# Two output weight tiles split in each block of the input projection instead of three, and one operand for the first half's sums of squares

## The chip, the cores and the metric

The kernel runs on one NeuronCore of a Trainium2 chip. Its engines are TensorE (PE in the profile, with its weight loads as PEld), VectorE (DVE), ScalarE (ACT), GpSimd (POOL) and SyncE (SP). SP issues nearly all DMAs here, in one queue and in order. The metric is device time in microseconds; the median of three runs of the kernel before is 2884.24 us (2881.09 to 2888.12).

## The reference

One inference step of a hybrid encoder layer, in fp32, over 2048 prompt frames and 32 frames of a running stream (2080 tokens), with D_MODEL 1024. A mixer runs stick-breaking attention (8 heads of 64) beside a Mamba-2 SSD (8 heads of 64, state 64, conv 4), both on one input projection; both results are normalised, concatenated and sent through one output projection; a gated conv feed-forward follows.

```python
def mixer(h, k_past, v_past, ssm_h0, conv_prev, p):
    proj = h @ p['w_in']
...
    attn = stick_breaking(q, q_pos, k_all, v_all, k_pos).reshape(b, l, D_ATT)
...
    y, h_fin = ssd_scan(xh, dt, a, bm, cm, ssm_h0.astype(jnp.float32))
...
    y = rmsnorm(y * jax.nn.silu(z), p['g_ssm_out'])
    out = jnp.concatenate([rmsnorm(attn, p['g_attn_out']), y], axis=-1) @ p['w_out']
    return out, k, v, h_fin.astype(ssm_h0.dtype), conv_new

def layer(x, k_past, v_past, ssm_h0, ssm_conv_prev, ffn_conv_prev, p):
    m, k, v, h_fin, ssm_conv_new = mixer(rmsnorm(x, p['g_mix_pre']), k_past, v_past, ssm_h0, ssm_conv_prev, p)
    x = x + rmsnorm(m, p['g_mix_post'])
    f, ffn_conv_new = conv_ffn(rmsnorm(x, p['g_ffn_pre']), ffn_conv_prev, p)
    x = x + rmsnorm(f, p['g_ffn_post'])
```

The change touches `w_out` (the output projection's weights) and the sums of squares of the two norms around `m` (`g_mix_post` and `g_ffn_pre`).

## The kernel before

**Arithmetic.** Every fp32 operand of a large matmul is split into a high and a low part (names ending in hi and lo, or the halves of a tile `w`); each product is three matmuls (hi by hi, hi by lo, lo by hi). So L180 (`dense`) issues three matmuls for each weight block of 128 by 128. Weights are split once: `divide` (L155) takes the raw fp32 tile (`wraw`, loaded in L137), casts the high part on ACT (L160), subtracts on POOL (L161) and stores both to DRAM (L164, `wS_...`). Every later use is a `recall` (L147), a load of the split tile (L152, `w<-wS_...`). `weight` (L122) picks one or the other by whether the key is in `kept`.

**Buffers and queue.** In the input projection the tiles `w` are of 1 MB and rotate through a ring of three buffers; behind it, of 512 KB in a ring of six. A load at the head of SP's queue waits there until its buffer is free, and everything issued behind it waits too.

**Input projection.** `phase_in` works through four blocks s of 512, 512, 512 and 544 tokens. In each: six tiles of conv, B, C and x; then v (L451, four steps b of 128 tokens, five in the last block, 48 matmuls each, copied out in L460, stored as `o_v` in L468 and, split, as `vS` in L476); then four tiles of wk and four of wq, from the ring; then the gate. Beside wk and wq run the SSD steps: step size and decay on DVE (L464 to L496, ending with `da`), cumulative sums on PE (L498, L499, copied to `acum` in L503), transposes (L509, L564, L575), the store of `acT` to `acD` and its broadcast load `acB` (L513, L520), and the products L581 and L593. The squares of the next block's x are added by POOL (L326). Ahead of a step of v, the kernel also splits one of the eight tiles of `wout`, for use in the streams much later; the cast is held behind the last copy of v by `behind`, an order on the engine without a wait.

**Streams.** Afterwards attention runs block by block (`heads`), and each block's tail (`Tail`) is interleaved with the attention of the next one; the last tail runs alone. A tail has two halves of up to 272 tokens. For each, `out_units` runs the eight tiles of the output projection (tile c of `wout`, copied to `m`, squared on ACT into `msq`, summed on POOL in `square`, L875), `residual` normalises and adds x, and `split` prepares the feed-forward. The sums of squares over the 1024 features reach PE as a list of operands of 128 rows: `rstd_steps` issues one matmul by a column of ones (L222) for each operand and each 128 tokens, adding in PSUM. The list is `self.msqs` for the first norm (two operands: `msq`, and the last square `sqt`) and `self.sq` for the second (two operands, `two[0]` with its two halves).

**Order.** The instruction order on each engine is decided by a scheduler from the program's order, its buffers and the explicit orders (`pin`, `behind`, `spaced`). A change of one line can therefore move instructions all over a block.

Of the kernel before, what the change touches and what calls it, by code (L numbers as in the profile page):

```python
# [12 lines left out]
ALU = mybir.AluOpType  # L13
# [21 lines left out]
KC = D // P  # L35
# [234 lines left out]
def phase_in(kn, ctx):  # L270
    nc, tc, a, o = kn.nc, kn.tc, kn.a, kn.o
# [7 lines left out]
    wp = kn.wp  # L279
# [94 lines left out]
    for s, (t0, nt) in enumerate(SBS):  # L374
# [18 lines left out]
        def silu(y, copy):  # L393
            t = tmp.tile([P, 550], F32, name="t")
            kn.behind(nc.scalar.activation(t[:, :W], y, AF.Sigmoid), copy)
            nc.vector.tensor_tensor(y, y, t[:, :W], op=ALU.mult)
# [44 lines left out]
            nc.vector.memset(u[:, 32:40], 0.0)  # L441
        for b in range(nb):
            q = min(P, nt - b * P)
            if 0 < s and 0 < b < 4 and 3 * s + b < KC + 4:
                kn.weight(wp, a["wout"][3 * s - 4 + b], key=("outw", 3 * s - 4 + b))
                kn.behind(kn.cast, copy)
            vp = [psd.tile([P, 512], F32, name="o") for _ in range(2)]
            for h in range(2):
                for k in range(KC):
                    for i, (l, rr) in enumerate(((xhi, wv[0]), (xlo, wv[0]), (xhi, wv[1]))):  # L450
                        nc.tensor.matmul(  # L451
                            vp[h][:q, :260], l[k][:, b * P : b * P + q], rr[:, k, h * 260 : h * 260 + 260],
                            start=i == 0 and k == 0, stop=i == 2 and k == KC - 1,
                        )
            v = sd.tile([P, 520], F32, name="v")
            for dst, src in ((v[:q, 0:260], vp[0][:q, :260]), (v[:q, 260:520], vp[1][:q, :260])):
                if s == 0:
                    copy = nc.scalar.activation(dst, src, AF.Copy, scale=rcol[:q, b : b + 1])
                else:
                    copy = nc.scalar.copy(dst, src)  # L460
            if b == 0:
                for y in owed:
                    silu(y, copy)
            nc.vector.tensor_tensor(  # L464
                u[:q, b * 8 : b * 8 + 8], v[:q, 512:520], kn.cv[:q, C_DTB : C_DTB + 8], op=ALU.add
            )
            tok = t0 + b * P
            nc.sync.dma_start(o["v"][tok : tok + q, :], v[:q, :512])  # L468
            if b == 4:
                nc.sync.dma_start(kn.vF[:], v[:DEC, :512])  # L470
                continue
            vs = sd.tile([P, 2, 512], F32R, name="vs", bufs=1)
            nc.gpsimd.tensor_copy(vs[:, 0, :], v[:, :512])
            nc.gpsimd.tensor_tensor(vs[:, 1, :], v[:, :512], vs[:, 0, :].bitcast(F32), op=ALU.subtract)
            for e in range(2):
                nc.sync.dma_start(  # L476
                    kn.vS[s][:, :, b, e * DH : e * DH + DH].rearrange("h p d -> p h d"),
                    vs[:, e, :].bitcast(F32).rearrange("p (h d) -> p h d", d=DH),
                )
# [512 lines left out]
class Tail:  # L992
# [24 lines left out]
    def out_units(self, s, cat, half):  # L1017

        kn, nc, att = self.kn, self.kn.nc, self.att
        c0, c1 = half  # L1020
        if c0 == 0:
            self.Q = [[self.mp.tile([P, 4, 272], F32, name=f"n{2 * i + e}") for e in range(2)] for i in range(2)]
            self.msq = att.tmp.tile([P, 544], F32, name="sq")
            self.w = {}
        back = list(range(KC - WBUFS * UNIT // KC, KC))
        for i, c in enumerate(range(KC) if c0 == 0 else back + list(range(back[0]))):
            m = self.m(c, half)
            w = self.w.pop(c, None)
            if w is None:
                pool = self.keep if self.keep is not None and c not in back else kn.wp  # L1030
                w = kn.weight(pool, kn.a["wout"][c], key=("outw", c, "part"), tag=f"w{c}" if pool is self.keep else None)
                if c0 == 0 and (c in back or pool is self.keep):
                    self.w[c] = w
            ps = self.po[0].tile([P, 512], F32, name=self.po[1])
            for k in (4, 5, 6, 7, 0, 1, 2, 3):
                kn.dense(ps, w[k : k + 1], cat, c0, c1, k0=k, first=k == 4, last=k == 3, pin=self.pin)
                if k != 3:
                    yield
            nc.scalar.copy(m, ps[:, : c1 - c0])
            if i < KC - 1:  # L1040
                att.square(self.msq[:, c0:c1], m, i == 0)
            else:
                t = att.tmp.tile([P, 272], F32, name="sqt", bufs=2)[:, : c1 - c0]
                nc.scalar.activation(t, m, AF.Square)
                self.msqs = [self.msq[:, c0:c1], t]
            yield
# [5 lines left out]
    def residual(self, s, half):  # L1052

        kn, nc, att = self.kn, self.kn.nc, self.att
        t0 = SBS[s][0]
        c0, c1 = half
        n = c1 - c0
        fast = s in FAST
        rm = kn.rstd_narrow(att.tmp, *kn.bank, self.msqs, n, D, stay=True)
        yield  # L1060
        self.h, two = [], []
        for c in range(KC):
            m = self.m(c, half)
            if c % 2 == 0:
                if self.late:
                    pair = self.late.tile([P, 548], F32, name="xr", bufs=4)
                else:
                    pair = self.yp.tile([P, 548], F32, name="gb") if c % 4 else self.yp.tile([P, 546], F32, name="y")
            x = pair[:, n * (c % 2) : n * (c % 2) + n]
            nc.sync.dma_start(x, kn.a["xT"][:, c, t0 + c0 : t0 + c1])  # L1070
            kn.spaced(nc.vector.scalar_tensor_tensor(
                m, m, kn.col(C_GMIXP + c), rm[:, :n], op0=ALU.mult, op1=ALU.mult
            ), self.pin)
            eng = nc.vector if c % 2 else nc.gpsimd
            h, sq = (x, m) if fast else (m, x)
            eng.tensor_tensor(h, m, x, op=ALU.add)
            nc.sync.dma_start(kn.hS[s][:, c, c0:c1], h)
            nc.scalar.activation(sq, h, AF.Square)
            self.h.append(h)
            if c % 2:  # L1080
                k = c % 4 - 1
                two.append(
                    self.Q[int(c0 > 0)][c // 4][:, k : k + 2, :n] if fast
                    else pair[:, : 2 * n].rearrange("p (k t) -> p k t", k=2)
                )
                if c > 1:
                    eng = nc.vector if fast and c0 and c == KC - 1 else nc.gpsimd
                    eng.tensor_tensor(two[0], two[0], two[-1], op=ALU.add)
            yield
        self.sq = [two[0][:, k, :] for k in range(2)]  # L1090

    def split(self, s, half):


        kn, nc, att = self.kn, self.kn.nc, self.att
        c0, c1 = half
        if c0 == 0:
            self.x = self.cat
        hi, lo = self.x
        for k in range(KC):  # L1100
            m = self.m(k, half)
            nc.scalar.activation(hi[k][:, c0:c1], m, AF.Copy, scale=kn.col(C_GFFN + k))
            kn.spaced(nc.vector.scalar_tensor_tensor(  # L1103
                lo[k][:, c0:c1], m, kn.col(C_GFFN + k), hi[k][:, c0:c1].bitcast(F32),
                op0=ALU.mult, op1=ALU.subtract,
            ), self.pin)
            yield
# [420 lines left out]
def build(nc, tc, a, o):  # L1528
    kn = Kernel(nc, tc, a, o)
    with ExitStack() as ctx:  # L1530
# [17 lines left out]
        with ExitStack() as c2:  # L1548
            kn.wp, kn.unit, kn.wbufs, kn.rbufs = c2.enter_context(tc.tile_pool(name="weights_in", bufs=1)), KC, 3, 2
            rest = phase_in(kn, c2)  # L1550
# [123 lines left out]
```

## Time and profile before

| | before |
|---|---|
| median of 3 runs | 2884.24 us |
| profiled execution | 2887.35 us |
| its span, first to last instruction | 2885.6 us |
| mean granted TensorE clock | 0.984 |
| HBM read, written | 482.40 MB, 156.57 MB |
| input projection, about | first 600 us of the span |

How to read the lines below: in the profile's groups and timelines a row names the start in us, the length, the engine (SPq is SP issuing a DMA), the line, the operation, the tile written and the tiles read, and a count; a bracket holds the idle time ahead of it and what ended it. A row of the list of waits is "engine, tile and line <- what it waited for: us in total, times, longest". A row of the chain of waits gives start, length and what took that stretch on the way to the end of the window. A row of the DMA list ends in KB and the median of the microseconds from issue to landing. `x19` counts instructions put together in one row.

### The profile page before, as it was taken

Reading aid. Unit: us, or ns where it says so; the run is one execution under the profiler, and the core shown is the slowest. Engines: PE = TensorE matmul, PEld = TensorE weight load, DVE = VectorE, ACT = ScalarE, POOL = GpSimd, SP = SyncE. Lnnn points to the kernel's source line nnn. Section 1 sums busy time; section 2 is a strip of 40 time slices with the busy share of each in tenths; the row PEclk is TensorE's granted clock in tenths of the full one; section 3 lists DMA queues with packets and bytes.
Section 4 is the critical chain, followed back from the end, with each engine's and each line's share of the span. In section 5 each row is a group of like instructions: output and inputs, shape, how many; then the busy total and the mean of one; then the engine's idle time right before and its main releaser. Section 6 shows DMA issues by size and latency. Waiting matters only on the chain.

```text
span 2885.6 us, 46011 instructions
## 1 busy us (share of the span) xinstructions
PE 2780.3 (96%) x16709; PEld 2401.0 (83%) x16709; DVE 1643.5 (57%) x2628; ACT 1217.0 (42%) x2568; POOL 1134.0 (39%) x1065
## 2 busy tenths in 40 slices
PE   7998999998999999999999999989999999999997
PEld 6777878986878888897888888878888879899997
DVE  7684747367464454558455555875666653623333
ACT  5343434347555454455333335644444433321111
POOL 4633242325566665556232224453323234411113
PEclk9999999999999999999999999999999999999999
DMA  8969595987768777886655556655555555755556
GB/s 295 290 248 332 199 315 194 280 276 252 249 206 281 275 265 257 268 268 217 201 180 183 175 180 237 206 191 185 176 168 171 167 187 175 247 179 179 167 179 200
DMA packets 348483, 642.02 MB, mean 222 GB/s; under 512 B 73338, under 2 KB 192770, under 8 KB 338530
## 3 DMA queue, kind: packets, MB, share of 16 engines
q1 hardware_dynamic: 348258, 639.09, 67.3%
q8 instruction: 133, 2.18, 0.3%
q14 instruction: 92, 0.75, 0.1%
HBM read 482.40 MB, written 156.57 MB: 221 GB/s over the span
## 4 chain that ended last, share of the span: by engine, by line
PE 79%; DMA 8%; DVE 7%; issue 2%; SPq 2%; POOL 1%; ACT 1%; DVEq 0%; ACTq 0%; POOLq 0%
PE o L180 41%; PE u L180 12%; PE t L180 10%; PE z L914 4%; PE pa L955 4%; PE pt L933 4%; PE o L451 2%; DMA acB<-acD 1%; DMA w<-wS_outw 1%; DVE prow L762 1%; DMA w<-wS_wk 1%; DMA w<-wS_up 1%; DVE f L1431 1%; DVE xlo L1103 1%; DMA k<-kS 1%
## 5 line engine op out<-in xcount | busy, mean ns | idle before, releaser
L180 PE MATMUL o<-xhi,w 128*128 128x512 f32 (+2 forms) x3968 | 1040.9, 344 | 26.3 <-ACT xhi L353 7.8
L180 PEld LDWEIGHTS o<-xhi,w 128*128 128x128 f32 x3968 | 694.9, 190 | 119.4 <-ACT xhi L353 7.8
L180 PE MATMUL o<-xlo,w 128*128 128x512 f32 (+2 forms) x1984 | 681.4, 344 | 5.1 <-DVE xlo L1103 2.2
L767 POOL TENSOR_TENSOR beta<-beta,prow 128x512 f32<-128x512 f32 (+3 forms) x256 | 255.5, 999 | 512.3 <-DVE prow L762 444.0
L180 PEld LDWEIGHTS o<-xlo,w 128*128 128x128 f32 x1984 | 377.1, 190 | 50.5 <-DVE xlo L1103 3.3
L180 PE MATMUL u<-xhi,w 128*128 128x512 f32 x1056 | 351.4, 398 | 0.0
L180 PE MATMUL o<-ah,w 128*128 128x512 f32 x992 | 342.1, 402 | 6.4 <-DVE f L1399 6.3
L1351 POOL TENSOR_TENSOR y<-y,gb 128x512 f32<-128x512 f32 (+1 forms) x88 | 116.1, 1320 | 460.6 <-ACT gb L1350 460.4
L938 DVE TENSOR_TENSOR wt<-pt,wt 128x512 fp32r<-128x512 f32 (+2 forms) x320 | 192.2, 602 | 182.9 <-ACT wt L937 181.0
L161 POOL TENSOR_TENSOR w<-wraw,w 128x512 fp32r<-128x512 f32 (+3 forms) x178 | 245.4, 1380 | 129.2 <-ACT w L160 105.4
L762 DVE TENSOR_TENSOR_SCAN prow<-gam,prow,z 128x513 f32<-128x513 f32 x192 | 245.2, 1277 | 54.3 <-ACT beta L760 53.6
L937 ACT CAST wt<-pt 128x512 fp32r<-128x512 f32 (+2 forms) x320 | 167.7, 525 | 233.1 <-PE pt L933 231.2
L180 PEld LDWEIGHTS u<-xhi,w 128*128 128x128 f32 x1056 | 199.0, 189 | 46.3
L180 PEld LDWEIGHTS o<-ah,w 128*128 128x128 f32 x992 | 186.7, 188 | 48.4 <-DVE f L1399 7.4
L180 PE MATMUL u<-xlo,w 128*128 128x512 f32 x528 | 209.3, 396 | 0.0
L759 ACT ACTIVATE gam<-z 128x512 f32<-128x512 f32 (+2 forms) x320 | 173.1, 541 | 60.7 <-PE z L914 35.2
L180 PE MATMUL t<-xhi,w 128*128 128x272 f32 x960 | 190.4, 294 | 7.6 <-DMA w<-wS_up 4.6
L180 PE MATMUL o<-al,w 128*128 128x512 f32 x496 | 196.6, 396 | 0.0
L933 PE MATMUL pt<-ident,beta 128*128 128x128 f32 x1088 | 184.6, 278 | 0.4 <-DVE wt L938 0.4
L955 PE MATMUL pa<-wt,v 128*64 128x256 f32 (+3 forms) x1152 | 173.5, 281 | 9.8 <-DVE wt L938 5.1
L160 ACT CAST w<-wraw 128x512 fp32r<-128x512 f32 (+3 forms) x178 | 113.0, 635 | 159.9 <-PE o L180 89.3
L1343 DVE SCALAR_TENSOR_TENSOR y<-gb,cv,y 128x512 f32<-128x512 f32 (+1 forms) x176 | 144.0, 818 | 63.9 <-ACT y L1341 60.8
(288 smaller groups left out, 4845.0 us busy)
## 6 DMA issues: line engine op xcount, KB each, us to landing
w<-wS_up SPq DMA_DIRECT2D x264, 512.0 KB, 3.6
w<-wS_dn SPq DMA_DIRECT2D x144, 384.0 KB, 3.4
w<-wS_outw SPq DMA_DIRECT2D x94, 512.0 KB, 6.2
wS_up<-w SPq DMA_DIRECT2D x88, 512.0 KB, 3.4
wraw<-wup SPq DMA_DIRECT2D x88, 256.0 KB, 4.4
k<-kS SPq DMA_DIRECT2D x80, 256.0 KB, 3.5
v<-vS SPq DMA_DIRECT2D x80, 256.0 KB, 3.7
w<-wS_bx SPq DMA_DIRECT2D x18, 1024.0 KB, 5.5
```

The costliest lines, as they stand in the source:

```text
L161: nc.gpsimd.tensor_tensor(lo, raw[:, :m, :], hi.bitcast(F32), op=ALU.subtract)
L180: mm = nc.tensor.matmul(ps[:, : c1 - c0], l, r, start=first and i == 0 and k == 0, stop=last and i == 2 and k == len(w) - 1, **({"skip_gro ...
L759: nc.scalar.activation(g[:, c0:512], z, AF.Sigmoid, scale=-0.125)
L762: nc.vector.tensor_tensor_scan(back(pr), back(g), z[:, 0:1].to_broadcast([P, n + 1]), self.kn.ones[:, 0:1] if prev is None else prev, op0= ...
L767: eng.tensor_tensor(b[:, :n], b[:, :n], pr[:, c0 + 1 : 513], op=ALU.mult)
L914: mm = nc.tensor.matmul(z[:, :n], q[:, P * b : P * b + P], k[:, :n], start=e == 0, stop=e == 1 and kc < s)
L933: mm = nc.tensor.transpose(t[:, P * j : P * j + P], w[:, P * j : P * j + P], kn.ident[:])
L937: nc.scalar.copy(hi, t)
L938: kn.exit = nc.vector.tensor_tensor(lo, t, hi.bitcast(F32), op=ALU.subtract)
L955: nc.tensor.matmul(av[:m, 2 * P * p + c0 : 2 * P * p + 2 * P], v[:, j, :m], wt[:, rest, j, c0:], start=kc == s and p + j + rest == 0, stop ...
L1343: nc.vector.scalar_tensor_tensor(y[:, :W], gb[:, i : i + W], kn.col(wc + i), y[:, :W], op0=ALU.mult, op1=ALU.add)
L1351: nc.gpsimd.tensor_tensor(y[:, :W], y[:, :W], t, op=ALU.mult)
```

## The change

Two edits.

1. In `phase_in`, blocks 1, 2 and 3 each split two tiles of `wout`, ahead of steps 1 and 2 of v: tiles 0 and 1, 2 and 3, 4 and 5. Before, blocks 1 and 2 split three each and block 3 two, all eight. Tiles 6 and 7 now have no key in `kept` when the first stream reaches them, so `weight` sends their four halves through `divide` there: a load of the raw half (prefetched), a cast, a subtraction and a store (`wS_outw_part`), where four recalls stood. Later streams recall those halves.
2. In `out_units`, for the first half of a stream (`c0 == 0`), the last square too is added to `msq` by `square`, so `msqs` is one operand. In `residual`, for the first half, POOL adds the second half of `two[0]` to the first, and `self.sq` is one operand. The second half of each stream is as before. This takes 18 matmuls of L222 away in the four streams and adds eight additions on POOL.

```diff
@@ -441,8 +441,8 @@
         for b in range(nb):
             q = min(P, nt - b * P)
-            if 0 < s and 0 < b < 4 and 3 * s + b < KC + 4:
-                kn.weight(wp, a["wout"][3 * s - 4 + b], key=("outw", 3 * s - 4 + b))
+            if 0 < s and 0 < b < 3:
+                kn.weight(wp, a["wout"][2 * s - 3 + b], key=("outw", 2 * s - 3 + b))
                 kn.behind(kn.cast, copy)
@@ -1037,8 +1037,9 @@
             nc.scalar.copy(m, ps[:, : c1 - c0])
-            if i < KC - 1:
+            if i < KC - 1 or c0 == 0:
                 att.square(self.msq[:, c0:c1], m, i == 0)
+                self.msqs = [self.msq[:, c0:c1]]
             else:
                 t = att.tmp.tile([P, 272], F32, name="sqt", bufs=2)[:, : c1 - c0]
@@ -1088,6 +1089,10 @@
         self.sq = [two[0][:, k, :] for k in range(2)]
+        if c0 == 0:
+            nc.gpsimd.tensor_tensor(self.sq[0], self.sq[0], self.sq[1], op=ALU.add)
+            del self.sq[1]
+            yield
```

The order of instructions moves with it. On SP, in block 1 from v's first stores on, before (`wS_outw_0_1926` and `wS_outw_0_1993` are the first two split tiles, `wS_wk_0_1074` and `wS_wk_0_1117` tiles 0 and 1 of wk):

```order
L476 DMA vS_87<-vs 128x8x64 x2
L468 DMA o_v<-v 128x512
L164 DMA wS_outw_0_1926<-w 128x2048
L137 DMA wraw<-wout 128x1024
L476 DMA vS_87<-vs 128x8x64
L164 DMA wS_outw_0_1993<-w 128x2048
L468 DMA o_v<-v 128x512
L152 DMA w<-wS_wk_0_1074 128x2048
L137 DMA wraw<-wout 128x1024
L476 DMA vS_87<-vs 128x8x64
L152 DMA w<-wS_wk_0_1117 128x2048
```

The same stretch now:

```order
L476 DMA vS_87<-vs 128x8x64 x2
L152 DMA w<-wS_wk_0_1074 128x2048
L468 DMA o_v<-v 128x512
L164 DMA wS_outw_0_1926<-w 128x2048
L137 DMA wraw<-wout 128x1024
L476 DMA vS_87<-vs 128x8x64
L164 DMA wS_outw_0_1993<-w 128x2048
L468 DMA o_v<-v 128x512
L137 DMA wraw<-wout 128x1024
L152 DMA w<-wS_wk_0_1117 128x2048
L476 DMA vS_87<-vs 128x8x64
```

The load of wk's tile 0 has moved from behind both stores to ahead of them, straight behind v's first two stores; that of tile 1 has moved ahead of one vS. Block 2 has the same two stretches with other numbers.

On PE, in block 1 at the end of wk's tile 0 (its 24 matmuls end with `xhi_1620` and `xlo_1628`), before:

```order
L180 MATMUL o<-xhi_1619,w 128x512
L498 MATMUL st<-da,triu 128x32
L499 MATMUL st<-da,ones 128x32
L180 MATMUL o<-xlo_1627,w 128x512
L180 MATMUL o<-xhi_1619,w 128x512
L180 MATMUL o<-xhi_1620,w 128x512
L180 MATMUL o<-xlo_1628,w 128x512
```

and now:

```order
L180 MATMUL o<-xlo_1628,w 128x512
L180 MATMUL o<-xhi_1620,w 128x512
L498 MATMUL st<-da,triu 128x32
L499 MATMUL st<-da,ones 128x32
L509 MATMUL st<-ident,acum 32x128
L564 MATMUL st<-ident,xc 128x128 x4
L575 MATMUL st<-ident,bc 128x128
```

The small matmuls stood between those of wk's tiles 0 and 1 (L509 another fifteen matmuls on, L575 directly ahead of L593); now all of them stand together between the two tiles, and L593 follows behind the 24 matmuls of tile 1.

On SP, in the first stream, at the recalls of the last tiles of the output projection's first half, now (before, this place had only recalls, of tiles 5, 6, 7 and then of the second half):

```order
L152 DMA w<-wS_outw_0_4789 128x2x512 x2
L164 DMA wS_outw_part_7628<-w 128x1024
L137 DMA wraw<-wup 128x512
L164 DMA wS_outw_part_7635<-w 128x1024
L137 DMA wraw<-wup 128x512
L164 DMA wS_outw_part_7692<-w 128x1024
L137 DMA wraw<-wup 128x512
L164 DMA wS_outw_part_7699<-w 128x1024
L137 DMA wraw<-wup 128x512
L152 DMA w<-wS_outw_0_1926 128x2x512 x2
```

Four stores, each followed by a load of a raw half tile of `wup`, stand where four recalls stood, ahead of the second half's recalls.

## The prediction

> **What bounds the kernel now.** I read the page first, for the engine that carries the span.
>
> ```profile
> PE 2780.3 (96%) x16709; PEld 2401.0 (83%) x16709; DVE 1643.5 (57%) x2628; ACT 1217.0 (42%) x2568; POOL 1134.0 (39%) x1065
> ```
>
> TensorE is busy for 2780.3 of 2885.6 us, so only about 105 us of the span is its idle time, and a change can win only in two ways: by closing idle stretches of PE, or by taking instructions off PE. The diff removes POOL, ACT and DMA work in blocks s=1 and s=2 of the input projection, so the second view is what PE waits for there, from 140 to 600 us (engine, line, releaser: us in total, times, longest).
>
> ```profile
> PE o L180 <- DMA w<-wS_wk: 7.3, 2, 3.9
> PE o L180 <- DMA w<-wS_wq: 3.0, 2, 2.1
> PE y L581 <- DVE acB L553: 2.5, 4, 1.5
> PE st L593 <- ACT bT L577: 1.7, 2, 0.8
> ```
>
> The largest are two waits for the first tile of wk. The timeline of PE says where (start, length, instruction, and in brackets the idle time before it with its releaser); the first row is in block 1, the others are in block 2.
>
> ```profile
> 228.50 0.77 PE L180 MATMUL o<-xhi,w 128*128 128x512 f32 x1 [3.92 <-DMA w<-wS_wk]
> 378.24 0.53 PE L180 MATMUL o<-xhi,w 128*128 128x512 f32 x1 [3.42 <-DMA w<-wS_wk]
> 414.22 0.66 PE L581 MATMUL y<-acB,xdt 128*64 128x128 f32 x8 [1.49 <-DVE acB L553]
> ```
>
> Blocks 1 and 2 split three output weight tiles, block 3 only two, and block 3 has no such wait. So the before trace already holds a sample of the changed form. The DMA queue's timeline shows why, block 1 first and block 3 below it.
>
> ```profile
> 207.36 2.02 SPq L476 DMA_DIRECT2D vS<-vs  x2
> 212.76 0.38 SPq L164 DMA_DIRECT2D wS_outw<-w  x1
> 219.31 1.22 SPq L152 DMA_DIRECT2D w<-wS_wk  x1
> ...
> 508.99 2.17 SPq L476 DMA_DIRECT2D vS<-vs  x2
> 511.25 2.66 SPq L152 DMA_DIRECT2D w<-wS_wk  x1
> 514.48 0.38 SPq L164 DMA_DIRECT2D wS_outw<-w  x1
> 523.47 0.85 SPq L152 DMA_DIRECT2D w<-wS_wk  x1
> ```
>
> The weight ring has three buffers. With three tiles split, wk's tile 0 takes the buffer of the first split tile and can be loaded only when that tile's store has landed; with two, it takes the third buffer and goes out right behind v's first stores (511.25, straight after 508.99). The chain of waits prices what a late load costs beyond the idle time itself.
>
> ```profile
> 219.31 9.05 DMA w<-wS_wk
> 228.50 6.16 PE o L180 x19
> 267.69 5.87 PE o L180 x24
> 276.63 4.43 PE o L180 x19
> 378.24 6.22 PE o L180 x19
> ```
>
> The same 19 matmuls take 6.16 and 6.22 us after the two gaps and 4.43 us elsewhere: 1.73 and 1.79 us more. The windows say that this is the granted clock (the columns are the busy times of PE, PEld, DVE, ACT and POOL, then clock, DMA share and GB/s).
>
> ```profile
> 224.00:236.00 12.00, 8.08 (x34) 6.43 (x33) 4.66 (x16) 5.92 (x9) 5.94 (x6) 0.86 1.05 370
> 513.00:530.00 17.00, 17.00 (x145) 16.54 (x145) 0.70 (x3) 2.83 (x6) 5.17 (x5) 1.00 0.98 324
> 727.00:750.00 23.00, 22.90 (x192) 22.50 (x191) 4.39 (x9) 8.81 (x24) 9.31 (x12) 1.00 0.64 218
> ```
>
> The clock is 0.86 behind the gap, 1.00 through v of block 3. A gap of 2.11 us (before 267.69) cost 5.87 against 4.43 x 24/19 = 5.60, only 0.27 us more.
>
> **The change, part by part.**
>
> *Third tile gone, block 1.* In the changed order wk tile 0 stands directly behind the first two vS stores, as in block 3. There it went out 2.26 us after them, so here at about 207.36 + 2.26 = 209.6; with 9.05 us it lands near 218.7, while v's last matmul ends near 224.57. The wait of 3.92 us goes with a margin of 5.9 us, and its 1.73 us of clock too: **5.65 us**. Next late is wk tile 1, whose buffer holds the first split tile until its store has landed.
>
> ```profile
> wS_outw<-w SPq DMA_DIRECT2D x8, 1024.0 KB, 8.4
> w<-wS_wk SPq DMA_DIRECT2D x12, 1024.0 KB, 8.3
> ```
>
> Store out at 212.76, landed at 221.2, load landed at 229.5. Tile 0's 24 matmuls take 5.60 us from 224.57, so tile 1 is needed at 230.2. By block 3's own rows (store 514.48, load 523.47: 9.0 us; store there 5.49 us behind vS, here at 212.85; load of 9.05) it lands at 230.9, 0.7 us late. I take 0.3 us of new wait, bounds 0 and 3. Queued behind that load, which holds the queue's head until 221.2 or so, are v's vS of step 2, o_v of step 3 and wk tiles 2 and 3; before, tile 1 itself left only at 224.49, so none of them is later than it was.
>
> By the Trainium skill (DMA: Bandwidth & Descriptors, "Anatomy of one DMA"), a DMA costs about 2.0 us plus its bytes at 436 GB/s, fitted on another issue path: 4.4 us for this store, an estimate from that page. By that tile 1 could never be late and the sum would be 0.3 us better per block; the trace differs, with 8.4 us at a DMA share of 1.05, and the measurement decides.
>
> *PE's order moves with it.* Until now part of the decay step's matmuls (L498, L499, L509) stood inside wk's tiles; now L498, L499 and L509 stand together behind tile 0, each waiting for a short DVE result.
>
> ```profile
> 224.59 0.95 DVE L464 TENSOR_TENSOR u<-v,cv 128x8 f32<-128x8 f32 x1 [4.88 <-ACT v L460]
> 229.84 0.19 DVE L496 TENSOR_TENSOR da<-dt,nega 128x32 f32<-128x32 f32 x1
> 234.63 0.39 PE L499 MATMUL st<-da,ones 128*128 128x32 f32 x2
> 235.05 0.19 DVE L503 COPY acum<-st 128x32 f32<-128x32 f32 x1 [5.02 <-PE st L499]
> ```
>
> da hangs on v, not on wk, so it is ready at 230.03 as before: level with PE's arrival at 230.2. L509 then needs acum, 235.24 minus 235.02 = 0.2 us after L499's end, plus its hand-over. I take 0.7 us of new waiting per block (bounds 0 and 1.5); queued behind L509 are four L564, one L575 and tile 1, so PE itself waits. For it, bT is transposed and copied 24 matmuls ahead of L593: its 0.8 us per block (1.7 in two, in the first list) goes.
>
> *The acB chain.* acD's store to DRAM now stands ahead of tile 0's kS stores rather than between kS stores. It left at 241.50 and acB's load at 251.79; both come some 10 us earlier: wk tiles 2 and 3 still stand ahead of acD, but tile 2's buffer needs only the second split tile's store to land and tile 3's the end of tile 0's matmuls at 230.2. This closes block 2's 1.49 us and block 1's 0.57:
>
> ```profile
> 263.47 0.66 PE L581 MATMUL y<-acB,xdt 128*64 128x128 f32 x8 [0.57 <-DVE acB L553]
> 267.69 0.50 PE L180 MATMUL o<-xhi,w 128*128 128x512 f32 x1 [2.11 <-DMA w<-wS_wq]
> ```
>
> The wq wait of block 1 stands in a stretch where DMA is full. A tile less means 512 KB of raw load, 1 MB of store: 1.5 MB, at the 370 GB/s of the window above 4.2 us of traffic less in front of it. But PE also arrives up to 8 us sooner, so I give it half of 2.11 + 0.27, 1.2 us (bounds 0 and 2.4).
>
> Block 1: 5.65 + 0.8 + 0.57 + 1.2 - 0.3 - 0.7 = 7.2. Block 2: 3.42 + 1.79 + 0.8 + 1.49 - 0.3 - 0.7 = 6.5. Together **13.7 us**. ACT and POOL work that goes there (a cast and a subtraction per block) frees no time of PE: no PE wait in the first list names them. The cover on the other side is DVE's preparation of the next block, which is tied to PE's gate matmuls and so moves with them.
>
> *Tiles 6 and 7 are split later*, in the first output stream, as four half tiles: four recalls become four casts, four subtractions and four 512 KB stores. Their raw halves take the place of wup's in the early prefetch.
>
> ```profile
> 605.75 4.69 SPq L137 DMA_DIRECT2D wraw<-wup  x5
> 727.39 30.25 SPq L152 DMA_DIRECT2D w<-wS_outw  x14
> 781.48 0.43 SPq L137 DMA_DIRECT2D wraw<-wup  x1
> 773.41 1.29 POOL L161 TENSOR_TENSOR w<-wraw,w 128x512 fp32r<-128x512 f32 x1
> ```
>
> Stores replace loads of equal size, and four wup loads of 256 KB move in between: 1 MB, 2.8 us of DMA time at 370 GB/s. The window 727 to 750 has a DMA share of 0.64, thus 8.3 us free, and POOL is busy 9.31 of 23 us, ACT 8.81, so four subtractions of 1.29 fit. I take 0 (bounds: 5 us gained, if the sixth wup raw, which left only at 781.48, now leaves earlier, and 5 us lost: the two longest single waits of 600 to 900 us, 2.5 each in the list below, once more).
>
> ```profile
> PE pa L955 <- ACT wt L937: 4.2, 3, 2.5
> PE z L812 <- DMA sk<-kF: 2.5, 1, 2.5
> ```
>
> *Squares.* Each of four streams drops two sets of 2 or 3 matmuls with one output column (L222): 18 in all. Eight POOL adds appear.
>
> ```profile
> 770.27 0.94 PE L222 MATMUL u<-ones,y 128*128 128x1 f32 x8
> L875 POOL TENSOR_TENSOR sq<-sq,sqt x72: 727/741/1185, 663.4 to 2433.5; 128x256 f32<-128x256 f32 x54, 128x272 f32<-128x272 f32 x18
> ```
>
> 0.94 / 8 = 0.12 us each, so 18 give **2.1 us**. The add of 0.74 us now stands between the last square and L222. In the streams that run beside attention the scheduler put L222 ten matmuls later, which covers it; with that cover gone in all eight places it would be 8 x 0.74 = 5.9 us. I take 0.7 us, one place in eight uncovered.
>
> By the Trainium skill (SBUF — State Buffer, "SBUF: two separate sides"), GpSimd and a two-input DVE operation share a port pair that one holds for its whole instruction, the other blocking. This speaks against moving sums from PE to POOL: in the worst case 8 adds would hold DVE for the same 5.9 us. The trace bears it out in part, with adds of 1185 ns beside a median of 741; the sum by it would be 5.2 us worse.
>
> Sum: 13.7 + 0 + 2.1 - 0.7 = **15.1 us**. The profiled execution took 2887.35 us (span 2885.6 and 1.75 around it), so it would be 2872.25; the runs' median, 2884.24, is 3.11 lower, and my forecast is 2884.24 - 15.1 = **2869.1**.
>
> **The rivals.**
>
> *Tile 1 of wk takes the wait over.* DMA is full in 224:236, and the load can only start when a store has landed. For it: 8.4 and 9.0 us stores; against it: 5.6 us of matmuls now stand in front. At 3 us late in each block, with clock, it gives back 2 x (3 + 1.75) = 9.5 us less the 0.6 counted: 2878.0.
>
> *Slower: the new stores stop the DMA queue in the first stream.* All transfers go through one queue in order. The four new stores stand ahead of the recalls of the second half; each waits for POOL's subtraction, which waits for ACT's cast, each in line behind attention. If each store holds the queue 4 us longer than its buffer's own wait, PE stops four times 4 us and pays 1.75 us of clock: 23 us, and the time is 2869.1 + 23 = 2892.1. It decides for slower from 21 us on, that is above 3.5 us per store. Against it: the queue already stood 30.25 us over 14 recalls there while PE was busy 22.90 of 23 us, so ring and prefetch give slack.
>
> *The sums come late.* All eight adds uncovered, each as slow as the slowest of that row (1185 ns): 9.5 us less the 0.7 counted: 2877.9. For it: nothing but POOL stands between the last square and L222; against it: POOL is busy for 39% of the span, so an add rarely finds it taken.
>
> *It doesn't do what it says*, the wk load staying behind the stores. The new DMA order excludes that for both blocks; I leave 1 in 100, with 2.1 - 0.7 us gained: 2882.8.
>
> **How the numbers follow.** Forecast as summed: 0.66. wk tile 1: 0.13. Sums late: 0.08. Stores stop the queue: 0.08. A lesser form of that, losing some 10 to 15 us and ending within 0.2% (5.8 us, about what a measurement of this kernel can tell from no change): 0.04. No effect: 0.01. Range: the gain is at most 15.1 + 0.3 x 2 + 0.7 x 2 + 1.2 + 5 + 0.7 = 24, thus 2860; the upper end, 2880, takes in wk tile 1 and late sums with a unit or two of their own spread. Faster than 2878.4: 0.66 + 0.13 + half of late sums, which end at that bound, = 0.83; same: 0.04 + 0.04 + 0.01 = 0.09; slower 0.08.
>
> **What would show it.** Right: the two PE waits for wS_wk gone, wk's first load right behind vS at about 210 us, the granted clock in the first 12 us of wk near 1.00, the acB waits gone, and 18 L222 fewer. wk tile 1 as the wait shows as a PE wait for wS_wk some 5.6 us behind v. The slower case shows as waits for w at L180 between 727 and 810 behind wS_outw_part stores. Waits of PE for POOL at L222 in four streams would mean that the sums are late. The forecast is wrong, too, if later streams, whose order also shifts, lose what the blocks win.

## The result and the profile after

| | before | changed |
|---|---|---|
| median | 2888.37 us (9 runs, 2881.09 to 2890.0) | 2872.6 us (9 runs, 2867.38 to 2883.05) |
| ratio | | 0.9949, 95% interval 0.9937 to 0.9962 |
| span of the profiled execution | 2885.6 us | 2870.8 us |
| mean granted clock | 0.984 | 0.984 |

By the ratio that is 14.7 us less (11.0 to 18.2), and the two profiled spans differ by 14.8 us. These lines answer the ones of before: PE's row of the page, then PE's waits from 140 to 600 us.

```profile
PE 2778.1 (97%) x16673; PEld 2399.6 (84%) x16673; DVE 1647.7 (57%) x2628; ACT 1217.1 (42%) x2570; POOL 1141.3 (40%) x1075
```

```profile
PE y L581 <- DVE acB L553: 3.9, 3, 2.5
PE st L564 <- DVE te L505: 3.0, 2, 1.5
...
PE o L180 <- DMA w<-wS_wq: 0.8, 1, 0.8
PE st L509 <- DVE acum L503: 0.6, 2, 0.3
```

PE is busy for about as long as before (2778.1 against 2780.3 us), so most of the gain is idle time that went. The two waits for wS_wk, 7.3 us, are gone from the list, and so is that for bT; at L564 a wait has come that was not there before, 3.0 us in two. The list seems to say that acB got worse (3.9 us against 2.5), but it covers more of the changed kernel: the longest of the three, 2.50 us, is block 3's, whose counterpart of 2.56 us stood at 601.53 before, outside of the window. In blocks 1 and 2 alone PE waited 2.1 us for acB before and 1.0 now.

The DMA queue's timeline in block 1 shows the load that moved (start, length of the issue, transfer).

```profile
207.72 2.03 SPq L476 DMA_DIRECT2D vS<-vs  x2
209.85 0.53 SPq L152 DMA_DIRECT2D w<-wS_wk  x1
212.68 0.35 SPq L468 DMA_DIRECT2D o_v<-v  x1
213.12 0.38 SPq L164 DMA_DIRECT2D wS_outw<-w  x1
...
220.92 1.16 SPq L152 DMA_DIRECT2D w<-wS_wk  x1
...
233.30 0.32 SPq L513 DMA_DIRECT2D acD<-acT  x1
...
246.76 0.58 SPq L520 DMA_DIRECT2D acB<-acD  x1
```

wk's tile 0 leaves at 209.85 instead of 219.31, tile 1 at 220.92 instead of 224.49. To see where the 14.8 us fell, the two traces are cut at events that both have. A block is counted from its first product with the low half of wv to that of the next block; block 3 ends at the first score of the sample attention, the first attention stage at its norm's first L222, the first stream at the norm of the next attention stage.

| stage | before | changed | difference |
|---|---|---|---|
| up to v of block 1 | 199.89 | 200.25 | +0.36 |
| block 1 | 150.24 | 144.73 | -5.51 |
| block 2 | 152.08 | 148.47 | -3.61 |
| block 3 | 115.85 | 114.94 | -0.91 |
| first attention stage | 96.79 | 96.40 | -0.39 |
| first stream | 502.90 | 500.72 | -2.18 |
| from there to the end | 1667.85 | 1665.29 | -2.56 |

Blocks 1 to 3 give 10.0 of 14.8 us. One profile of a stage carries its own scatter: in e_sq below, whose instruction order in the blocks is that of before, block 1 took 148.54 and block 2 157.72 us; in e_after, the changed kernel's program once more, the last stage of the table took 1674.8 us, 9.5 more than here. So the differences of the last two rows are too small for one profile to show.

### The profile page after: what moved, and what is told of

Same layout as the page of the kernel before. It is cut to its first block, busy times and chain, and to the rows that moved or that the text cites. A ratio compares the mean times of both kernels' runs of the same rounds, so it can differ in the third digit from the quotient of the medians.

```text
span 2870.8 us, 45929 instructions
## 1 busy us (share of the span) xinstructions
PE 2778.1 (97%) x16673; PEld 2399.6 (84%) x16673; DVE 1647.7 (57%) x2628; ACT 1217.1 (42%) x2570; POOL 1141.3 (40%) x1075
## 3 DMA queue, kind: packets, MB, share of 16 engines
q8 instruction: 133, 2.18, 0.3%
## 4 chain that ended last, share of the span: by engine, by line
PE 81%; DVE 7%; DMA 6%; issue 2%; ACT 2%; POOL 1%; SPq 1%; DVEq 0%; ACTq 0%; POOLq 0%
PE o L180 41%; PE u L180 12%; PE t L180 11%; PE z L914 4%; PE pa L955 4%; PE pt L933 4%; PE o L451 2%; DMA acB<-acD 1%; DMA w<-wS_outw 1%; DVE prow L762 1%; DVE xlo L1108 1%; DVE f L1436 1%; DMA w<-wS_up 1%; DMA w<-wS_wq 1%; PE u L222 1%
```

## The experiments

Of the kernels below, the first four shared a chip and 23 runs of the kernel before, the next four another and 31 runs, the last three a third and 17 runs. Ratios are to the kernel before on the same chip.

### e_two: the first edit alone

```diff
-            if 0 < s and 0 < b < 4 and 3 * s + b < KC + 4:
-                kn.weight(wp, a["wout"][3 * s - 4 + b], key=("outw", 3 * s - 4 + b))
+            if 0 < s and 0 < b < 3:
+                kn.weight(wp, a["wout"][2 * s - 3 + b], key=("outw", 2 * s - 3 + b))
```

> The change's first edit alone (two output weight tiles per block, tiles 6 and 7 split in the first stream), sums of squares as before. Theory: the input projection wins about 10 us (the two waits for wS_wk with their slow clock gone, a new wait at L564 of about 1.5 us in blocks 1 and 2), and the later streams little, so 9 to 12 us faster than before. Rival: the streams' gain of about 5 us comes from the new places of the split, too; then 14 to 15 us faster.

Measured: 0.9951 (0.9937 to 0.9965), 2877.75 us against 2889.78. Blocks 1 and 2 took 144.64 and 148.43 us, as in the changed kernel. The first edit carries most of the gain. By the ratio it is 14.2 us, nearer to the rival's figure; the interval (10.1 to 18.2) holds both the rival's 14 to 15 us and most of the theory's 9 to 12, so it does not decide between them.

### e_sq: the second edit alone

```diff
-            if i < KC - 1:
+            if i < KC - 1 or c0 == 0:
                 att.square(self.msq[:, c0:c1], m, i == 0)
+                self.msqs = [self.msq[:, c0:c1]]
...
+        if c0 == 0:
+            nc.gpsimd.tensor_tensor(self.sq[0], self.sq[0], self.sq[1], op=ALU.add)
+            del self.sq[1]
+            yield
```

> The second edit alone (one operand for the first half's sums), three tiles per block as before. Theory: 18 matmuls of 0.12 us less and hardly an add uncovered: 1 to 4 us faster than before, PE's waits for wS_wk of 3.9 and 3.4 us still there. Rival: the eight adds come late and take back what the matmuls give: within 1 us, with PE waits for POOL at L222 in the four streams.

Measured: 0.9990 (0.9980 to 1.0000), 2.9 us faster, between 5.8 and nothing. That is the theory's size, at the edge of what can be told from no change. PE still stopped at wk's first tile, for 3.2 us in block 1 and 2.1 in block 2, less than the 3.9 and 3.4 expected. The list of waits puts these stops down to ACT instructions (L488, L486); the tile's load left behind both stores as before, at 220.43 and 368.97, and in block 2 it landed 7.2 us later, 0.1 us before PE went on.

### e_hoist: three tiles, but wk's first load written early

```diff
+            if 0 < s < 3 and b == 3:
+                wk0 = kn.weight(wp, a["wk"][0], key=("wk", 0))
             if 0 < s and 0 < b < 4 and 3 * s + b < KC + 4:
                 kn.weight(wp, a["wout"][3 * s - 4 + b], key=("outw", 3 * s - 4 + b))
...
-                w = kn.weight(wp, a[name][c], key=(name, c))
+                w = wk0 if name == "wk" and c == 0 and 0 < s < 3 else kn.weight(wp, a[name][c], key=(name, c))
```

> Both edits' sums, but three tiles per block as before, with the load of wk's tile 0 written ahead of the third split in blocks 1 and 2, so that it stands directly behind v's first two vS stores in the DMA queue, as in the changed kernel, while the third tile's 512 KB raw load, cast, subtraction and 1 MB store stay. Theory (the load's place in the queue is what costs, not the third tile's traffic): the two waits for wS_wk at wk tile 0 are gone, and the time is within 4 us of the changed kernel. Rival (traffic and buffers of the third tile): DMA stays full, wk tile 0 or tile 1 waits 2 to 4 us per block, and the time is that of the second edit alone.

Measured: 0.9995 (0.9986 to 1.0005): no gain beside e_sq's. Both sides missed: the theory the time, the rival, whose time it is, the waits. The load left at 209.87 and PE waits for wS_wk nowhere in the blocks, yet blocks 1 and 2 took 150.57 and 149.70 us. The rows of PE and POOL in block 1 say what is late instead (L595 is L593 of the kernel before, L573 its L571).

```profile
234.06 0.42 PE L577 MATMUL st<-ident,bc 128*128 128x128 f32 x1
238.28 1.12 PE L595 MATMUL st<-xw,bT 128*64 128x256 f32 x4 [3.79 <-POOL xw L573]
```

```profile
223.16 2.39 POOL L161 TENSOR_TENSOR w<-wraw,w 128x1024 fp32r<-128x1024 f32 x1 [1.73 <-ACT w L160]
...
234.69 1.27 POOL L476 TENSOR_TENSOR vs<-v,vs 128x512 fp32r<-128x512 f32 x1
237.18 1.04 POOL L573 TENSOR_TENSOR xw<-xdt,te 128x512 f32<-128x512 f32 x1 [1.23 <-DVE xdt L568]
```

With a third tile the scheduler puts the state product (L595) directly behind the transpose L577, ahead of wk tile 1; in the changed kernel the 24 matmuls of tile 1 stand between the two. PE then stops for xw for 3.79 us, and the clock in the 5 us behind it is 0.50. In block 2 that wait is only 0.7 us, and the block 1.2 us longer than the changed kernel's.

### e_dec: the decay's exponential ahead of the copy of wk's first tile

```diff
-        nc.scalar.activation(dec[:, :n8], ps[:, 64 : 64 + n8], AF.Exp)
+        decay = nc.scalar.activation(dec[:, :n8], ps[:, 64 : 64 + n8], AF.Exp)
...
-                    leave(kf[:, c0:c1], ps[:, :n], c0, c1)
+                    out = leave(kf[:, c0:c1], ps[:, :n], c0, c1)
+                    if name == "wk" and c == 0 and 0 < s < 3:
+                        kn.behind(out, decay)
```

(`leave` now returns its ACT instruction.)

> The changed kernel with the copy of wk's first tile (L371) ordered behind the decay's exponential (L504) on ACT in blocks 1 and 2. Theory: the new wait of PE at L564 (1.48 us in both blocks) is ACT's table load, 1.28 us, which now starts only behind that copy; ordered ahead of it, it runs while ACT is idle, L564 waits 0.3 us or less, and block 2 keeps its clock: 2 to 4 us faster than the changed kernel. Rival: the copy comes later by as much, and PE stops for it or for what it feeds (kS stores, the next PSUM buffer): no gain, within 1 us.

Measured: 0.9951 (0.9939 to 0.9964), no gain over the changed kernel. The wait at L564 fell from 3.0 to 0.3 us in two, and blocks 1 and 2 took 142.66 and 146.53 us, 4.0 less than the changed kernel's. But the scheduler's order behind them changed as well, and the first attention stage took 101.71 us instead of 96.40. The wait's cause stood confirmed, its worth in time did not; e_warm, below, leaves the orders of PE and DMA queue alone.

### e_hold, e_traffic, e_ring4: buffer, traffic or place in the queue

e_hold takes a buffer of the ring without traffic, e_traffic brings the traffic without a buffer, and e_ring4 gives the kernel before a fourth buffer.

```diff
+            if 0 < s < 3 and b == 3:
+                kn.hold = kn.held(wp, None)
+                nc.scalar.copy(kn.hold[:, 0, 0, 0:1], kn.ones[:, 0:1])
```

```diff
                 kn.behind(kn.cast, copy)
+                if b == 2 and s < 3:
+                    spare = kn.dp.tile([P, 2, KC, P], F32, name="spare")
+                    nc.sync.dma_start(spare[:], kn.wlast[:].bitcast(F32))
+                    kn.raw(a["wout"][6 + s - 1], KC)
```

```diff
-            kn.wp, kn.unit, kn.wbufs, kn.rbufs = c2.enter_context(tc.tile_pool(name="weights_in", bufs=1)), KC, 3, 2
+            kn.wp, kn.unit, kn.wbufs, kn.rbufs = c2.enter_context(tc.tile_pool(name="weights_in", bufs=1)), KC, 4, 2
```

> The changed kernel, but in blocks 1 and 2 a third buffer of the weight ring is taken ahead of v's last step by a cast of one column, with no load, subtraction or store: wk's tile 0 then has to take the first split tile's buffer, as it did before. Theory (the third tile's claim on the ring sets where wk's first load stands in the queue): the load moves behind the first store and the second raw load and waits there for that store to land, some 8.4 us; it goes out at about 221, lands at 229 to 230 and PE waits 3 to 5 us for wS_wk again in both blocks, though nothing of the third tile's traffic is there. 7 to 12 us slower than the changed kernel. Rival (traffic): no wait for wS_wk, time as the changed kernel within 2 us.

> The changed kernel with the third tile's traffic put back in blocks 1 and 2 without its buffer: the second split tile is stored a second time (1 MB) and one more raw tile is loaded (512 KB) and not used. Theory (place in the queue): wk's tile 0 still goes out at about 210 and PE doesn't wait for it; wk tile 1 may come 1 to 2 us late, so 0 to 4 us slower than the changed kernel. Rival (traffic): PE waits 3 us and more for wS_wk in both blocks, 7 us and more slower.

> The kernel before, with four ring buffers instead of three in the input projection: wk's tile 0 needs none of the split tiles' buffers, but its load stands in the queue where it stood, behind both stores and v's third o_v. Theory (place in the queue, not a wait for the buffer on the chip): the load goes out at about 219 and PE waits 3 to 4 us for wS_wk in both blocks as before. Rival (buffer): the waits are gone, 9 us and more faster than before.

Measured: e_hold 1.0003 (0.9991 to 1.0016), e_traffic 0.9998 (0.9988 to 1.0009), e_ring4 1.0004 (0.9990 to 1.0018). All three have lost the gain, or never had it, and for three different reasons.

e_ring4 decides its question. There the load of tile 0 waits on the semaphores of PE and of the eighth transfer ahead of it in the queue, and on no store of a split tile; still it stands behind both stores, and PE waits as before. The DMA queue in block 1, then PE's waits from 140 to 600 us:

```profile
214.44 0.32 SPq L164 DMA_DIRECT2D wS_outw<-w  x1
217.33 0.34 SPq L468 DMA_DIRECT2D o_v<-v  x1
217.76 2.54 SPq L152 DMA_DIRECT2D w<-wS_wk  x2
```

```profile
PE o L180 <- DMA w<-wS_wk: 7.0, 2, 3.9
```

The load leaves 0.43 us behind the o_v ahead of it, as it did before (219.31 behind 218.87). So on the chip it is the place in the queue that makes tile 0 late, not the buffer's release. The time of e_ring4 says less, since other instructions moved with the fourth buffer: its block 1 took 145.72 us, its block 2 157.89.

e_hold did not do what it was made for: the third buffer was handed to wk's tile 0 itself, so that its load left at 214.84, behind the first store (213.87) and one raw load, with no wait for that store. PE did not wait for it, but 10.3 us for acB instead of 3.9 (both lists from 140 to 600 us), and the first attention stage took 103.67 us instead of 96.40. On the buffer it tells nothing.

In e_traffic the load left at 209.23 and PE waited for no wS_wk, as the theory said; but it was not 0 to 4 us slower, it was some 14. As in e_hoist the scheduler moved the state product (here L598) ahead of wk tile 1:

```profile
PE st L598 <- POOL xw L576: 6.8, 2, 3.4
PE st L569 <- DVE te L510: 3.0, 2, 1.5
```

Its blocks took 149.66 and 154.06 us, with a clock of 0.54 and 0.50 in the 5 us behind the two waits for xw. Neither side foresaw this. What the traffic alone would cost at an unchanged order stays open.

### e_late: tiles 6 and 7 in block 3

```diff
-            if 0 < s and 0 < b < 3:
+            if 0 < s and 0 < b < (5 if last else 3):
                 kn.weight(wp, a["wout"][2 * s - 3 + b], key=("outw", 2 * s - 3 + b))
```

> The changed kernel with tiles 6 and 7 split in block 3 of the input projection, ahead of v's steps 3 and 4, instead of in the first stream; four recalls stand there again. In block 3 wk's first load then stands behind three stores, later by some 14 us than in the changed kernel. Theory: splitting in the first stream costs nothing, and block 3 pays a wait for wS_wk of 0 to 3 us: 0 to 5 us slower than the changed kernel. Rival: the split in the first stream costs 3 us or more there (1 MB more of traffic, ACT and POOL in line): faster than the changed kernel by 2 us or more.

Measured: 0.9992 (0.9982 to 1.0003), so some 12 us of the gain are lost, more than either side expected. Blocks 1 and 2 kept it (145.40 and 146.88 us), block 3 took 124.66 us instead of 114.94. Its DMA queue and PE's waits there, from 480 to 640 us:

```profile
516.03 0.32 SPq L164 DMA_DIRECT2D wS_outw<-w  x1
517.33 1.13 SPq L152 DMA_DIRECT2D w<-wS_wk  x1
```

```profile
PE y L581 <- DVE acB L553: 7.1, 3, 3.4
PE o L180 <- DMA w<-wS_wk: 3.9, 1, 3.9
PE st L593 <- POOL xw L571: 1.5, 1, 1.5
```

So in block 3, too, wk's first load goes behind the stores when more than two tiles are split there. With four tiles it cost 9.7 us of that block; with three, blocks 1 and 2 lost 11.0 us together (below). And the four recalls that came back into the first stream gained nothing there worth mentioning: it took 499.67 us against 500.72.

### e_after, e_warm, e_place: the changed kernel beside two edits of it

e_warm adds an exponential whose result nothing reads, so that ACT loads its table earlier; e_place puts wk's first load back behind the second store, with two tiles.

```diff
-        nc.scalar.activation(lw[:, :n8], ab[:, :n8], AF.Ln)
+        ln = nc.scalar.activation(lw[:, :n8], ab[:, :n8], AF.Ln)
+        if 0 < s < 3:
+            warm = tiny("warm")
+            kn.behind(nc.scalar.activation(warm[:, 0:1], kn.ones[:, 0:1], AF.Exp), ln)
```

```diff
                 w = kn.weight(wp, a[name][c], key=(name, c))
+                if 0 < s < 3 and name == "wk" and c == 0:
+                    kn.behind(kn.got, store)
```

(`store` is the second split tile's store, `kn.got` the recall's load.)

> The changed kernel once more, beside the two below on one chip and against the kernel before. Both theories: 0.994 to 0.996 of before, and in its trace blocks 1 and 2 (from v's first matmul to that of the next block) of 144 to 146 and 148 to 149 us, with L564 waiting 1.48 us in both.

> The changed kernel with one more ACT instruction in blocks 1 and 2: an exponential of one column, ordered behind the logarithm of the step size (L488), whose result nothing reads. PE's and the DMA queue's orders are those of the changed kernel, row for row. Theory (PE's new wait at L564 is ACT's load of the exponential's table, 1.28 us, behind the copy of wk's first tile): the load now falls into ACT's idle time ahead of that copy, L564's wait falls from 1.48 to about 0.2 us in both blocks, block 2 may keep its clock: 2 to 4 us faster than the changed kernel. Rival (what e_dec suggested: shorter blocks only let PE run into the next wait): the wait at L564 goes, but waits at acB, wq or in the first stream grow by as much, within 1 us of the changed kernel.

> The changed kernel (two tiles per block) with wk's first load ordered behind the second split tile's store in blocks 1 and 2, where it stood before; no third raw load, cast, subtraction or store there. Theory (the load's place in the queue is what the change gains by): the load goes out at about 219.5 in block 1, PE waits 2.5 to 4 us for wS_wk in both blocks and loses 1.7 us of clock behind it: 6 to 11 us slower than the changed kernel. Rival (the third tile's traffic and its ACT and POOL work): with 1.5 MB less in front the load lands in 5 to 6 us, PE waits 1 us or less: within 3 us of the changed kernel.

Measured: e_after 0.9946 (0.9933 to 0.9960), e_warm 0.9946 (0.9933 to 0.9960), e_place 1.0012 (1.0002 to 1.0023).

e_place undoes the change's whole gain without a third tile: 19 us slower than e_after (2894.56 against 2875.24), where the theory expected 6 to 11 and the rival 3 at most. Its DMA queue in block 1 and PE's waits from 140 to 600 us:

```profile
218.84 0.34 SPq L469 DMA_DIRECT2D o_v<-v  x1
219.27 2.45 SPq L152 DMA_DIRECT2D w<-wS_wk  x2
```

```profile
PE o L180 <- DMA w<-wS_wk: 5.8, 2, 3.1
PE y L582 <- DVE acB L554: 3.5, 2, 2.6
PE st L594 <- POOL xw L572: 2.1, 1, 2.1
PE st L576 <- DVE hT L606: 1.6, 1, 1.6
```

The wait for wS_wk is back in both blocks, as the theory said. But of the 19 us the blocks hold only 5.0 (150.02 + 148.70 against e_after's 146.83 + 146.88), and not all of these are the load's: with the order that the scheduler built around it, pauses for xw and hT came to block 1 (2.1 and 1.6 us), and L564's went. The first attention stage took 106.71 us against 96.24, again in an order that the scheduler had shifted, at a mean clock of 0.84 against 0.93. So putting the load back brings its wait back, and with the order that is built on it the whole gain goes; what the place alone is worth, at an unchanged order, is not shown. The clock behind the two waits for wS_wk, 1.00 over 5 us, had no part in it; behind that for xw it was 0.50.

e_after's blocks, at 146.83 and 146.88 us, both fell outside of what was expected: block 1 waited 1.39 us for acB, with a clock of 0.68 in the 5 us behind it, and block 2 kept a clock of 1.00 behind L564.

e_warm answers the question of L564. ACT in block 1 of the changed kernel, then of e_warm, where L507 is L504:

```profile
230.77 0.59 ACT L371 COPY kf<-o 128x512 f32<-128x512 f32 x1 [2.22 <-PE o L180]
231.37 1.28 ACT L504 ACT_TABLE_LOAD   x1
232.67 0.20 ACT L504 ACTIVATE dec<-st 128x32 f32<-128x32 f32 x1
```

```profile
228.61 1.28 ACT L491 ACT_TABLE_LOAD   x1
229.90 0.20 ACT L491 ACTIVATE warm<-ones 128x1 f32<-128x1 f32 x1
230.82 0.58 ACT L371 COPY kf<-o 128x512 f32<-128x512 f32 x1 [0.71 <-PE o L180]
231.41 0.20 ACT L507 ACTIVATE dec<-st 128x32 f32<-128x32 f32 x1
```

The exponential comes 1.26 us sooner, and PE's waits, from 140 to 600 us, show it:

```profile
PE y L584 <- DVE acB L556: 5.2, 4, 2.4
PE o L180 <- DMA w<-wS_wq: 2.0, 3, 1.0
...
PE st L567 <- DVE te L508: 0.3, 2, 0.2
```

Blocks 1 and 2 took 290.5 us together, against 293.7 in e_after and 293.2 in the changed kernel's first profile. In the time nothing of these 3 us shows: 2875.39 us against 2875.24, within an interval of about 4 us. So the wait's cause is shown; whether its removal is worth 3 us or is taken back by acB (5.2 us here, 3.9 and 4.6 in the two profiles of the changed kernel) is not decided.

## Why the prediction was right

The forecast was 15.1 us less, the ratio says 14.7 (11.0 to 18.2), and the main step went as forecast: wk's first load moved, and PE's two waits for it went. That the sum is as close as 0.4 us is luck. The blocks were taken at 13.7 us and gave 11.0, the squares at 1.4 and gave 2.9, and the two errors cancel in part.

**wk's first load.** Right: it left at 209.85 (209.6 forecast), the waits of 3.92 and 3.42 us are gone, and the clock from 224 to 236 us, 0.86 before, is 1.00. In e_place, where the load stands behind the stores again without a third tile, both waits are back.

**The reason given for it** was wrong in one point. The prediction said that tile 0 "can be loaded only when that tile's store has landed". It put that landing at 221.2, with the median of 8.4 us for such a store. The buffer was indeed that of the first split tile, and the load does wait for its store; but this store, out at 212.76, took only 5.2 us in the trace of before:

```profile
DMA to landing us min/median/max: 5.2/5.2/5.2
```

So it had landed at 218.0, 1.3 us before the load left at 219.31, directly behind o_v at 218.87 (in block 2 at 368.9, before 369.56): the queue's order held the load, not a wait. In e_ring4 a load that waits for no store left just as closely behind o_v, and PE waited 7.0 us where it had waited 7.3. Three tiles instead of two change the order that the scheduler builds, and the wait follows from the order.

**Tile 1** left at 220.92 (221.2 to 221.9 forecast), landed 8.4 us later, and PE did not wait for it; the 0.3 us per block were not needed.

**The decay matmuls** are a term that was mis-sized: 0.7 us per block was taken, with 1.5 as the bound. L509 waits 0.28 us, as reckoned from acum. What was missed stands behind it: PE's timeline first, then DVE's.

```profile
233.14 0.66 PE L564 MATMUL st<-ident,xc 128*128 128x128 f32 x4 [1.48 <-DVE te L505]
```

```profile
232.90 0.19 DVE L505 TENSOR_TENSOR te<-st,acum 128x32 f32<-128x32 f32 x1 [1.57 <-ACT dec L504]
```

L564 writes a PSUM buffer that te still has to read; te waits for dec, and dec now stands behind the copy of wk's tile 0 and a table load. Before, that table load ran while ACT was idle. Together 1.76 us per block, 2.1 us more in two than was taken, and in block 2 the clock fell behind it to 0.66 in two of three profiles with this order (below), another 1.1 us: 24 matmuls took 6.72 us there and 5.61 in block 1.

```profile
233.91 5.61 PE o L180 x24
...
379.09 6.72 PE o L180 x24
```

**acB and wq.** acD left 8.2 us earlier (233.30), acB 5.0 us (246.76), not "some 10". The two waits for acB that were named are gone, but one of 1.00 us came later in block 1. The wq wait of 2.11 us went wholly where half was taken. Blocks 1 and 2 gave 9.1 us in the first pair of profiles where 13.7 were forecast; taking e_sq as a second profile of before, and e_two and e_after with the changed kernel, it is 304.3 against 293.3, 11.0 us.

**Tiles 6 and 7** in the first stream were taken at nothing, and no cost shows: that stream is 2.18 us shorter (4.2 in e_two, without the second edit), and PE's wait for w<-wS_outw between 700 and 830 us fell from 1.3 us to this row:

```profile
PE o L180 <- DMA w<-wS_outw: 0.2, 1, 0.2
```

The slower rival, stores that stop the queue, did not happen: the first and the last of the four stores left 4.9 us apart.

```profile
727.36 0.33 SPq L164 DMA_DIRECT2D wS_outw_part<-w  x1
...
732.23 0.65 SPq L164 DMA_DIRECT2D wS_outw_part<-w  x1
```

**The squares** were taken at 2.1 - 0.7 = 1.4 us; e_sq has 2.9 (nothing to 5.8). The first term was miscounted. A matmul of L222 leaves two rows in these traces: the row of eight that was priced at 0.94 us stands for two operands on two times 128 tokens, that is four matmuls, and PE's instructions fall by 36 (x16709 to x16673) for the 18 matmuls that went. At the same 0.94 / 8 us per row the term is 4.2 us, and the sum for the squares 3.5. From 600 us to the end PE waits at L222 for one POOL add, of fsq, as long as before (2.0 us); the rival of late sums did not happen either.

```profile
PE u L222 <- POOL fsq L875: 2.0, 1, 2.0
```

The Trainium skill's rule on the port pair of GpSimd and DVE (SBUF — State Buffer, "SBUF: two separate sides") had spoken against the adds; no run here shows that it cost anything: the group of the adds (shortest, median and longest in ns), which holds four of the eight new ones, reaches 974 ns, where it reached 1185 before, and the other four took 734 to 974 ns.

```profile
L875 POOL TENSOR_TENSOR sq<-sq,sqt x76: 726/742/974, 652.6 to 2418.7; 128x256 f32<-128x256 f32 x57, 128x272 f32<-128x272 f32 x19
```

**What stays open** is where the rest of the gain lies. Behind the blocks' 11.0 us the ratio leaves 3.7, and its interval (11.0 to 18.2) is as wide as that on either side. e_sq's 2.9 would fill most of that, but e_two, without the squares, has 14.2 us by its ratio. The profiles cannot place it: from the end of the first stream to the end of the span the kernel before took 1667.85 us, the changed kernel 1665.29, e_two 1665.6, and e_after, the changed kernel's program again, 1674.8.

## What to carry to other kernels

Where a scheduler sets the order, one more piece of work ahead of a load can move that load behind stores, and the wait follows from its place in the in-order queue, though every buffer is free: compare the order rows of a neighbouring stage that has the lighter form. An edit that takes one wait away regroups what follows; look for the next operand of each regrouped matmul, its PSUM buffer's last reader included, and follow that reader to a table load. Before pricing an instruction by a row of the profile, check how many rows one of it leaves. And price an experiment by stage: three of the edits here (e_hold, e_dec, e_place) lengthened the first attention stage, 200 us and more behind the edit, by 5 to 10 us.

## What the runs showed of the hardware that was not expected

How long a pause of PE has to be before the granted clock falls is no fixed figure here. The prediction took a pause of 2.11 us as harmless and those of 3.4 us and more as costing 1.7 to 1.8 us. The windows over the 5 us behind a pause (columns as in the prediction: five busy times, then clock, DMA share, GB/s) show 0.66 behind L564's 1.48 us in block 2 of the changed kernel, and 1.00 behind the same pause in block 2 of e_after:

```profile
377.90:382.90 5.00, 5.00 (x18) 4.15 (x19) 3.04 (x10) 0.58 (x3) 3.15 (x4) 0.66 0.89 321
```

```profile
380.00:385.00 5.00, 4.97 (x24) 4.15 (x25) 3.11 (x10) 0.64 (x3) 3.09 (x4) 1.00 0.89 326
```

In e_place, pauses of 2.69 and 3.13 us were followed by 1.00; the first of them:

```profile
227.20:232.20 5.00, 4.96 (x23) 4.09 (x24) 1.18 (x6) 2.22 (x3) 0.00 (x0) 1.00 1.06 377
```

A pause of 2.07 us in e_sq was followed by 0.66, and those of 3.02 us and 3.94 us in e_ring4 by 0.66 as well. Behind the first 20 us of the 13 profiles here, the 35 pauses of 3.16 us or more all had a clock of 0.70 or less over the 5 us behind them; shorter ones, down to the 1.39 us in e_after, went either way, for one program and one place too.
